# Batched 64x64 matmul: another order of issue for the b tiles, an early table load, a regroup in pieces and a store in halves

## The chip, the cores and the metric

One core of a Trainium2 chip runs the whole program. The metric is device time in microseconds (us), as the median of several executions. "Span" is the length of the one profiled execution, from its first to its last instruction; it is some 2 us shorter than the timed figure of the same program.

## The reference

```python
a = np.random.randn(1024, 64, 64).astype(np.float32)
b = np.random.randn(1024, 64, 64).astype(np.float32)
def reference(a, b):
    return np.matmul(a, b).astype(np.float32)
```

This reads 33.6 MB and writes 16.8 MB. The kernel computes in bf16: a is cast by its loads, b by ScalarE.

## The kernel before

b and the output are cut into 16 tiles t of 1.05 MB, a into 8 tiles s that serve two t each. The path of a tile of a: four loads issued by GpSimd (which cast it to bf16); a *regroup* on VectorE (DVE); transposes on TensorE; copies `at_sb` on ScalarE (ACT); then, for each t, four copies (*spread*) on DVE into a block-diagonal `at_bd`. b is loaded, then cast by ACT. TensorE leaves the products in PSUM; they are copied out of it (*evacuated*), first half of a tile by ACT and second half by DVE, and stored by GpSimd.

```python
    def load_b(t):
        b_sb = b_pool.tile([128, 16, 128], fp32, name="b_sb")       # 4 buffers
        queue = nc.scalar if t in (1, 3, 5, 7) else nc.sync
        load = queue.dma_start(out=b_sb[:], in_=b_v[t])
        # ... tiles 0 and 1 wait for the second piece of a tile 0 ...
    def regroup(s):
        # ...
        nc.vector.tensor_copy(a_bf[:], a_sb[:].rearrange("p h v k -> p v h k"))
    # ... in multiply(t), after the products:
            if not last:
                copy = nc.vector.tensor_copy if half else nc.scalar.copy
                evacuate(o_ps, 4 * half, 4, copy)
        if last:      # t == 15
            held[t] = [lambda q=q: put(2 * q, 2) for q in range(4)]
        else:
            held[t] = [lambda: put(0, 8)]
    # ... main loop (cut):
        for t in range(n_t):
            if t + 1 < n_t:
                spread(t + 1); cast(t + 1)
            if t + B_AHEAD < n_t:
                load_b(t + B_AHEAD)
            if half == 0:
                # ... regroup(s + 2), load_a(s + 4) ...
            multiply(t)
            # ... transpose ...
            if t >= HOLD - 1:
                store(t - HOLD + 1)
```

Every engine takes its instructions in this order. A load of b on ScalarE's queue therefore goes out only after the cast in front of it has got its data (in the prediction's lines a cast waits until 33.27 us, and the load of b tile 5 behind it goes out at 33.35). There are three DMA queues: q0 (loads of a and all stores, from GpSimd), q1 (b tiles from SyncE) and q10 (b tiles from ScalarE).

## Time and profile before

| | before |
|---|---|
| median of 4 runs | 137.08 us (136.76 to 137.43) |
| span of the profiled run | 134.8 us |
| busy: DVE, ACT, TensorE | 105.0, 84.5, 69.3 us |
| last store issued by GpSimd | 128.23 us (128.21 in the prediction, where the queue's own 0.02 us is counted in), landed 5.1 us later |

The slices, the stops of DVE and the queues are read in the prediction below. One view is shown here: how the end looks in single microseconds. The columns are the stretch, its length, the busy time of PE (TensorE), PEld (its weight loads), DVE, ACT and POOL (GpSimd) with numbers of instructions, TensorE's granted clock, the busy share of the 16 DMA engines and GB/s.

```profile
123.00:124.00 1.00, 1.00 (x24) 1.00 (x22) 0.97 (x3) 0.78 (x3) 0.00 (x0) 0.50 0.92 360
124.00:125.00 1.00, 0.45 (x9) 0.28 (x6) 0.96 (x3) 0.97 (x3) 0.04 (x1) 0.50 0.53 201
125.00:126.00 1.00, 0.00 (x0) 0.00 (x0) 0.97 (x3) 0.13 (x1) 1.00 (x2) 0.50 0.10 29
126.00:127.00 1.00, 0.00 (x0) 0.00 (x0) 0.96 (x3) 0.00 (x0) 1.00 (x2) 0.50 0.59 209
132.00:133.00 1.00, 0.00 (x0) 0.00 (x0) 0.00 (x0) 0.00 (x0) 0.00 (x0) 0.50 0.75 262
```

### The profile page before, as it was taken

The numbers are of one execution on the slowest core, as the hardware profiler recorded it, in microseconds if no ns is written. First come the engines' busy times: TensorE is split into PE (matmuls) and PEld (weight loads), VectorE is DVE, ScalarE is ACT, GpSimd is POOL, SyncE is SP. The second block draws the span as 40 slices with busy tenths as digits, with TensorE's granted clock in tenths as the row PEclk, the third lists the DMA queues.
The fourth block names the chain that finished last, engine by engine and source line by source line (L and its number), as shares of the span: only waits on it lengthen the run. The fifth ranks groups of instructions, "written<-read, shape, count | busy, mean of one in ns | idle before, by whom it ended". The sixth has DMA issues, their size and how long they took to land.

```text
span 134.8 us, 2815 instructions
## 1 busy us (share of the span) xinstructions
PE 69.3 (51%) x1152; PEld 65.2 (48%) x1152; DVE 105.0 (78%) x143; ACT 84.5 (63%) x122; POOL 46.6 (35%) x58
## 2 busy tenths in 40 slices
PE   0007305695169709389637861956039735669000
PEld 0007205695069609289637861956039625558000
DVE  5512099069999999997999999997599999999900
ACT  0010902992998995958996896699347996637100
POOL 6949723132413350152322243323021114040820
PEclk9999999999955995955995599599955995555555
DMA  2999999999999999999999999999999999998593
GB/s 19 185 204 261 309 305 301 309 308 279 272 294 311 312 394 346 303 275 361 393 360 273 272 381 396 340 267 288 393 394 396 393 399 395 407 406 350 191 320 136
DMA packets 17469, 42.12 MB, mean 312 GB/s; under 512 B 1073, under 2 KB 1073, under 8 KB 17457
## 3 DMA queue, kind: packets, MB, share of 16 engines
q0 software_dynamic: 9008, 25.17, 66.1%
q1 hardware_dynamic: 6336, 12.58, 26.0%
q10 hardware_dynamic: 2112, 4.19, 8.1%
q8 instruction: 9, 0.15, 0.4%
q14 instruction: 4, 0.02, 0.0%
HBM read 33.55 MB, written 16.78 MB: 373 GB/s over the span
## 4 chain that ended last, share of the span: by engine, by line
DMA 65%; DVE 18%; issue 9%; POOL 3%; POOLq 1%; DVEq 0%
DMA a_sb<-in_a_dram 48%; DMA out_dram<-o_sb 16%; DVE o_sb L157 10%; DVE at_bd L113 8%; POOL out_dram L146 2%; POOL a_sb L66 1%; POOLq L250 1%; DVE a_bf L91 0%; DVEq L91 0%; POOLq L146 0%; DVEq L113 0%; POOLq L239 0%
## 5 line engine op out<-in xcount | busy, mean ns | idle before, releaser
L169 PEld LDWEIGHTS <-at_bd 128*128 128x128 bf16 x1024 | 45.8, 117 | 41.4 <-DVE o_sb L157 30.7
L169 PE MATMUL o_ps<-b_bf,at_bd 128*128 128x64 bf16 x960 | 44.7, 219 | 36.6 <-DVE o_sb L157 28.7
L113 DVE COPY at_bd<-at_sb 32x1024 f32<-32x1024 f32 x64 | 46.4, 725 | 7.9 <-ACT at_sb L103 5.9
L157 DVE COPY o_sb<-o_ps 64x512 f32<-64x512 f32 x60 | 41.3, 688 | 1.8 <-PE o_ps L169 0.8
L157 ACT COPY o_sb<-o_ps 64x512 f32<-64x512 f32 x60 | 34.8, 580 | 9.5 <-DMA out_dram<-o_sb 5.3
L146 POOL DMA_DIRECT2D out_dram<-o_sb x19 | 21.0, 1107 | 46.9 <-DVE o_sb L157 20.1
L124 ACT CAST b_bf<-b_sb 128x2048 bf16<-128x2048 f32 x15 | 28.6, 1905 | 8.7 <-DMA b_sb<-in_b_dram 8.5
L66 POOL DMA_DIRECT2D a_sb<-in_a_dram x32 | 21.5, 681 | 35.2 <-DMA a_sb<-in_a_dram 21.0
L100 PE MATMUL at_ps<-identity,a_bf 128*128 128x128 f32 x128 | 24.4, 357 | 17.3 <-DVE a_bf L91 17.3
L100 PEld LDWEIGHTS at_ps<-identity,a_bf 128*128 128x128 f32 x128 | 20.5, 190 | 17.7 <-issue 17.7
L103 ACT COPY at_sb<-at_ps 128x512 f32<-128x512 f32 x32 | 17.6, 589 | 4.8 <-PE at_ps L100 4.5
L91 DVE COPY a_bf<-a_sb 128x4096 bf16<-128x4096 bf16 x8 | 9.8, 1228 | 11.5 <-DMA a_sb<-in_a_dram 11.3
L76 ACT MOVE_SHAPE b_sb<-in_b_dram x4 | 0.7, 172 | 7.9 <-DMA a_sb<-in_a_dram 7.0
L157 ACT COPY o_sb<-at_ps 64x256 f32<-64x256 f32 x8 | 2.9, 367 | 3.0 <-PE at_ps L169 2.9
L191 DVE MEMSET at_bd<- 128x4096 f32 x1 | 3.5, 3472 | 1.7 <-PEq L239 1.7
L103 ACT ACT_TABLE_LOAD x1 | 1.3, 1283 | 4.8 <-issue 4.8
L169 PE MATMUL at_ps<-b_bf,at_bd 128*128 128x64 bf16 x64 | 3.6, 241 | 1.2 <-DVE at_bd L113 1.2
L195 POOL MEMSET at_bd<- 128x4096 f32 x1 | 3.5, 3530 | 0.0
L157 DVE COPY o_sb<-at_ps 64x256 f32<-64x256 f32 x8 | 3.4, 421 | 0.1
L131 ACT CAST b_bf<-b_sb 128x512 bf16<-128x512 f32 x2 | 1.1, 615 | 1.9 <-DMA b_sb<-in_b_dram 1.9
L129 DVE CAST b_bf<-b_sb 128x512 bf16<-128x512 f32 x2 | 0.8, 424 | 0.0
masks.py:199 POOL TENSOR_SCALAR_AFFINE_SELECT identity<-identity 128x128 f32<-128x128 f32 x1 | 0.3, 287 | 0.1
(5 smaller groups left out, 0.6 us busy)
## 6 DMA issues: line engine op xcount, KB each, us to landing
out_dram<-o_sb POOLq DMA_DIRECT2D x15, 1024.0 KB, 21.8
a_sb<-in_a_dram POOLq DMA_DIRECT2D x32, 256.0 KB, 19.8
out_dram<-o_sb POOLq DMA_DIRECT2D x4, 256.0 KB, 5.3
b_sb<-in_b_dram SPq DMA_DIRECT2D x12, 0.5 KB, 18.3
b_sb<-in_b_dram ACTq DMA_DIRECT2D x4, 0.5 KB, 16.0
```

Source lines behind the costliest of these rows:

```text
L66: load = nc.gpsimd.dma_start(out=a_sb[:, h, :, :].rearrange("p v k -> p (v k)"), in_=a_v[s, h])
L91: nc.vector.tensor_copy(a_bf[:], a_sb[:].rearrange("p h v k -> p v h k"))
L100: nc.tensor.transpose(at_ps[:, vo, :], a_cols[:, 4 * vo + 2 * j + wl, :], identity[:])
L103: nc.scalar.copy(at_tiles[s][:, j, :, wl, :, :], at_ps[:].rearrange("p vo (g mp) -> p g mp vo", mp=4),)
L113: nc.vector.tensor_copy(bd[rows, :, :, :, h, :].rearrange("p j g wl mo -> p j (g wl) mo"), at_tiles[t // 2][rows, :, half, :, :, :].rearrange(
L124: nc.scalar.copy(b_bf[:], b_sb[:])
L146: nc.gpsimd.dma_start(out=o_v[t, :, lo : lo + n, :], in_=o_sb[:, lo : lo + n].rearrange("p gh j wl n -> p (gh j wl n)"),)
L157: copy(dst, src)
L169: nc.tensor.matmul(o_ps[:, gl, g % 2, j, :], at_bd[:, j, g, :, u], b_bf[:, g, 64 * u : 64 * u + 64], start=(u == 0), stop=(u == 1),)
L191: nc.vector.memset(bd_tiles[0][:], 0.0)
L195: nc.gpsimd.memset(bd_tiles[1][:], 0.0)
L250: with _tile.TileContext(nc) as tc:
```

## The change

The intent: free ScalarE at the head (its second load of b held it for 4.77 us, and its table load came after that), start the transposes of the first tile earlier, and let half of tile 14 be stored before DVE has evacuated the rest.

```diff
+    warm = consts.tile([128, 2], fp32)
@@ load_b
-        queue = nc.scalar if t in (1, 3, 5, 7) else nc.sync
+        queue = nc.scalar if t in (1, 4, 6, 7) else nc.sync
@@ regroup
-        nc.vector.tensor_copy(a_bf[:], a_sb[:].rearrange("p h v k -> p v h k"))
+        for lo, hi in [(0, 1), (1, 2), (2, 3), (3, 4)] if s == 0 else [(0, 4)]:
+            nc.vector.tensor_copy(
+                a_bf[:, :, lo:hi, :],
+                a_sb[:, lo:hi, :, :].rearrange("p h v k -> p v h k"),
+            )
@@ multiply
-            held[t] = [lambda: put(0, 8)]
+            whole = t < n_t - 2
+            held[t] = [lambda q=q: put(q, 8 if whole else 4) for q in ([0] if whole else [0, 4])]
@@ after load_a(0)
+        nc.vector.memset(warm[:, 0:1], 0.0)
+        nc.scalar.copy(warm[:, 1:2], warm[:, 0:1])
```

## The prediction

> **What bounds the kernel now.** I read the page's forty slices first, to see which resource is full and when.
>
> ```profile
> DVE  5512099069999999997999999997599999999900
> ACT  0010902992998995958996896699347996637100
> DMA  2999999999999999999999999999999999998593
> ```
>
> A slice is 134.8 / 40 = 3.37 us. The DMA row is full from slice 1 to slice 35, about 3.4 to 121 us; DVE is nearly full from slice 9 to slice 37; ACT is not. So a shorter instruction pays only if it fills an empty DMA slice or moves the DVE stream. Next, the timeline of DVE, for the places where it stops. Columns: start, length, instruction, in brackets the idle time before it and what ended it.
>
> ```profile
> 9.60 1.23 DVE L91 COPY a_bf<-a_sb 128x4096 bf16<-128x4096 bf16 x1 [4.47 <-DMA a_sb<-in_a_dram]
> 16.75 2.83 DVE L113 COPY at_bd<-at_sb 32x1024 f32<-32x1024 f32 x4 [5.92 <-ACT at_sb L103]
> 28.10 1.23 DVE L91 COPY a_bf<-a_sb 128x4096 bf16<-128x4096 bf16 x1 [4.51 <-DMA a_sb<-in_a_dram]
> 45.18 2.83 DVE L113 COPY at_bd<-at_sb 32x1024 f32<-32x1024 f32 x4
> 95.80 1.23 DVE L91 COPY a_bf<-a_sb 128x4096 bf16<-128x4096 bf16 x1 [2.33 <-DMA a_sb<-in_a_dram]
> 124.45 3.48 DVE L157 COPY o_sb<-at_ps 64x256 f32<-64x256 f32 x8
> ```
>
> After 28.1 us DVE runs to 127.93 us with one large stop, 2.33 us at 95.80, for the last tile of a (tile 7). From there 32.1 us of DVE work follow, almost without a gap, then the last stores. The end is therefore: landing of a tile 7, plus 32.1 us, plus the tail of the stores. Third, ScalarE at the head:
>
> ```profile
> 8.56 4.77 ACTq L76 DMA_DIRECT2D b_sb<-in_b_dram  x1
> 13.37 1.28 ACT L103 ACT_TABLE_LOAD   x1 [4.83 <-issue]
> 22.72 1.90 ACT L124 CAST b_bf<-b_sb 128x2048 bf16<-128x2048 f32 x1 [6.01 <-DMA b_sb<-in_b_dram]
> 33.27 1.90 ACT L124 CAST b_bf<-b_sb 128x2048 bf16<-128x2048 f32 x1 [2.54 <-DMA b_sb<-in_b_dram]
> ```
>
> ACT is held 4.77 us by issuing b tile 3 and then loads its table, but a little later it waits 6.01 us for b tile 0 anyway. Fourth, the DMA queues in 1 us stretches (packets, MB, share), 43 to 44 us and then 33 to 34 us:
>
> ```profile
> q0 software_dynamic: 50, 0.09, 45.6%
> q1 hardware_dynamic: 54, 0.11, 31.8%
> q10 hardware_dynamic: 52, 0.11, 27.3%
> ...
> q0 software_dynamic: 67, 0.13, 70.0%
> q1 hardware_dynamic: 66, 0.14, 39.5%
> q10 hardware_dynamic: 1, 0.00, 0.1%
> ```
>
> q0 carries a and the stores, q1 the b tiles of SyncE, q10 those of ScalarE. Queues with work get equal numbers of packets: with q10 empty, q0 gets 67 per us instead of 50. Last, the stretches of the end (length; PE, PEld, DVE, ACT, POOL; clock, DMA share, GB/s):
>
> ```profile
> 114.00:120.00 6.00, 3.78 (x64) 3.46 (x64) 5.80 (x9) 3.46 (x6) 1.36 (x1) 0.50 1.03 405
> 120.00:125.00 5.00, 3.59 (x64) 3.43 (x64) 4.82 (x10) 2.80 (x8) 0.04 (x1) 0.50 0.90 352
> 125.00:128.20 3.20, 0.00 (x0) 0.00 (x0) 2.83 (x7) 0.13 (x1) 2.97 (x4) 0.50 0.59 200
> ```
>
> Here is the hole: before the last two stores the DMA falls to 200 GB/s (in single microseconds 201, 29 and 209 from 124 to 127), because the store of tile 14 is issued whole at 124.97.
>
> **What the Trainium skill says.** "DMA: Bandwidth & Descriptors", section "Queues, rings and completion order": each DMA engine goes round robin between the queues with work, by packet. The trace agrees (50, 54, 52; then 67, 66). Same page, "Latency and other measured facts": about 600 ns to the first byte on the SyncE/ScalarE path. This trace differs: b tile 5 was issued on ScalarE at 33.35 and q10 moved no data before about 37.9, some 4.5 us; b tiles 0 and 1 (issued 7.03) started at about 11.5. I use 4.5. "ScalarE: Activation LUTs", "What ACT_TABLE_LOAD costs": about 1283 ns; the trace has 1283. "VectorE: DVE Perf Modes", "Side-by-side: where the cycles go": a 4x bf16 copy costs elements/4 plus about 158 cycles at 0.96 GHz; 4096 elements make 1231 ns, the trace has 1228. A quarter should cost 414 / 0.96 = 431 ns (an estimate from that section).
>
> **The change, part by part.**
>
> 1. *Table early.* One tiny memset and copy are added; the 1.28 us load moves into ACT's first 7 us, where it is idle. 2. *Four-piece regroup.* 1.23 us becomes 4 x 0.43 us, three of them while later pieces of the tile still land. Transposes can start about 10.1 instead of 10.98. 3. *b tile 3 to SyncE:* ACT loses its 4.77 us block. Together the four copies of at_sb end near 14.4 instead of 16.71, since the 16 transposes take 3.65 us and the last copy 0.6; spread 0 ends near 17.3 instead of 19.58. None of this reaches the end by itself: the first products still need b tile 0 (landed 22.7) and its cast (24.6), and DVE still stops for a tile 2. So I put 0 us on parts 1 and 2.
>
> 4. *The new order of b.* Before: q1 has 0, 2, 4, 6, 8...; q10 has 1, 3, 5, 7. After: q1 has 0, 2, 3, 5, 8...; q10 has 1, 4, 6, 7. Data of b tiles 0 and 1 is through by about 22. Tile 4 can be issued by ACT only beside its second cast (25.5), with data at about 30, so q10 is empty for 8 us where tile 3 now follows at once. Then q0 moves about 70 packets per us instead of 50: the last two pieces of a tile 2 (256 packets) take 3.7 instead of 5.1 us, and it lands near 26.5 instead of 28.0. b tile 2 has q1's larger share too and lands near 30 instead of 33.2. DVE restarts about 1.2 us earlier (its next evacuation needs products that end at 28.1).
>
> The price: b tile 3 is now behind tile 2 on q1 and shares with tile 4, at 33 packets per engine and 52/16 = 3.25 per us: 10.2 us, landing near 40.4 (its cast was at 38.42). ACT works in order: cast 1.9, four evacuations 2.4, two at_sb copies 1.1, so spread 4 starts near 46 instead of 45.18. DVE ends that passage 0.8 us late. It has 2.33 us of slack at 95.8.
>
> Over the whole run, q10 is busy beside q1 for fewer microseconds: before 11.5 to 32.1 and 37.9 to 59.1, 41.8 us; after about 11.5 to 22, 30 to 40.4, 45 to 49 and 52 to 65, some 38 us. In each of the 4 us saved q0 moves 18 packets more; 72 packets at 68 per us are 1.1 us. a tile 7 lands near 94.6, DVE is ready for it near 94.3, and the last 32.1 us begin about 1.1 us earlier.
>
> 5. *Tile 14 in halves.* Its first half (0.52 MB) is evacuated by ACT at 119.19 and can be issued then, 5 us ahead. It fills the hole: 0.52 MB no longer stand behind 124.97, at the 340 GB/s of the last stores 1.5 us. One DVE spread then coincides with a store's issue and stretches from 0.69 to 0.95 us (as others do now): +0.26.
>
> Sum: -1.1 - 1.5 + 0.3 = -2.3 us, 134.7. I put 134.8, as such gains seldom come whole.
>
> **The rivals.** (a) *Only the tail counts:* the late b tile 3 and the early a tiles cancel; a tile 7 lands as now, because the DMA is full and moves the same bytes. Then -1.2: 135.8. For it: the full DMA row. Against: the equal shares, which favour q0 when q10 is empty. (b) *The wait for b tile 3 takes the place of the removed one:* ACT stops for 4 to 5 us, evacuations and stores shift, and the 2.33 us of slack do not cover it, +1 in place of -1.1: about 136.8. For it: only 1 us lies between the last at_sb copy (44.15) and spread 4 (45.18). (c) *All is recovered:* the DMA never runs dry at the end, which the hole of about 0.76 MB against 400 GB/s allows, 1.9 us, and the start comes 1.5 us earlier: 133.6. (d) *Everything hidden,* because the last piece of tile 15, issued at 128.21 and gated by DVE, sets the end and not the queue ahead of it. Against: its 5.1 us from issue to landing are mostly queue. 137.
>
> **Range and chances.** (a) and the sum are likeliest, (c) less so, (b) and (d) least. That spans 133.4 to 136.4. The line for faster is 0.98 x 137.04 = 134.3, half a microsecond under my figure: 0.34. Slower than 139.8 needs a wait nothing shows: 0.02.
>
> **What would show it.** Part 1 to 3: ACT's table load before 7 us, at_sb copies ended near 14.4, and still a wait for b tile 0 until about 22.7. Part 4: DVE's regroup of a tile 2 near 26.6, ACT's fourth cast waiting for DMA until about 40.5, spread 4 near 46, the regroup of a tile 7 near 94.7. Part 5: a store issued near 119 and no microsecond under 300 GB/s between 120 and 128. I am wrong if the fourth cast waits much beyond 42 and DVE reaches a tile 7 later than 95.8, or if the last stretch from DVE's end to the end of the span (6.9 us) does not shrink.

## The result, and the profile after

| | before | changed |
|---|---|---|
| median | 137.08 us (4 runs) | 135.59 us (4 runs, 135.51 to 135.68) |
| ratio | | 0.9891, 95% interval 0.9865 to 0.9916 |
| span of the profiled run | 134.8 us | 133.8 us |
| DVE starts the last regroup (a tile 7) | 95.80 us | 94.98 us |
| DVE ends | 127.93 us | 127.14 us |
| last store issued | 128.23 us | 127.43 us |

A ratio here is the mean time of one kernel's runs over that of the other's of the same rounds, so it is not quite the ratio of the medians. The change is worth 1.5 us (1.1%): within 2%, and in the range. The figure forecast was 134.8.

The timeline of DVE in the changed kernel, the lines that answer to those of the prediction:

```profile
9.41 0.43 DVE L94 COPY a_bf<-a_sb 128x1024 bf16<-128x1024 bf16 x1 [0.82 <-DMA a_sb<-in_a_dram]
14.29 2.83 DVE L119 COPY at_bd<-at_sb 32x1024 f32<-32x1024 f32 x4 [4.45 <-ACT at_sb L109]
26.97 1.23 DVE L94 COPY a_bf<-a_sb 128x4096 bf16<-128x4096 bf16 x1 [5.39 <-DMA a_sb<-in_a_dram]
45.71 3.15 DVE L119 COPY at_bd<-at_sb 32x1024 f32<-32x1024 f32 x4 [1.81 <-ACT at_sb L109]
94.98 1.23 DVE L94 COPY a_bf<-a_sb 128x4096 bf16<-128x4096 bf16 x1 [1.53 <-DMA a_sb<-in_a_dram]
123.65 3.49 DVE L163 COPY o_sb<-at_ps 64x256 f32<-64x256 f32 x8
```

The first spread is 2.5 us earlier, and DVE waits the longer for a tile 2, which comes 1.1 us earlier. At 45.71 there is a new stop of 1.81 us. The last regroup starts 0.8 us earlier. ScalarE in the changed kernel:

```profile
0.74 1.28 ACT L198 ACT_TABLE_LOAD   x1 [0.74 <-PEq L249]
22.47 1.90 ACT L130 CAST b_bf<-b_sb 128x2048 bf16<-128x2048 f32 x1 [8.21 <-DMA b_sb<-in_b_dram]
40.42 1.90 ACT L130 CAST b_bf<-b_sb 128x2048 bf16<-128x2048 f32 x1 [4.73 <-DMA b_sb<-in_b_dram]
117.92 1.14 ACT L137 CAST b_bf<-b_sb 128x512 bf16<-128x512 f32 x2 [3.68 <-DMA b_sb<-in_b_dram]
```

The table load is out of the way of the copies of `at_sb`, and the wait for b tile 0 has grown from 6.01 to 8.21 us: the time saved at the head went into that wait. The fourth line is one that the prediction did not have: b tile 15 arrives at 117.9 instead of 115.2. The queues of the changed kernel from 25 to 26 us, where before all three had 49 packets each:

```profile
q0 software_dynamic: 74, 0.12, 66.3%
q1 hardware_dynamic: 73, 0.15, 42.8%
```

q10 is empty here, as b tile 4 was issued at 24.45 and no packet of it moved before 28.6. Last the end, GpSimd's issues of stores and then the stretches (columns as above):

```profile
121.73 0.77 POOL L152 DMA_DIRECT2D out_dram<-o_sb  x1 [2.94 <-ACT o_sb L163]
123.91 1.46 POOL L152 DMA_DIRECT2D out_dram<-o_sb  x2 [1.42 <-DVE o_sb L163]
125.67 1.43 POOL L152 DMA_DIRECT2D out_dram<-o_sb  x2 [0.30 <-DVE o_sb L163]
127.43 0.72 POOL L152 DMA_DIRECT2D out_dram<-o_sb  x1 [0.33 <-DVE o_sb L163]
```

```profile
125.00:126.00 1.00, 0.00 (x0) 0.00 (x0) 0.95 (x3) 0.00 (x0) 0.69 (x2) 0.50 0.95 361
130.00:131.00 1.00, 0.00 (x0) 0.00 (x0) 0.00 (x0) 0.00 (x0) 0.00 (x0) 0.50 0.45 172
131.00:132.00 1.00, 0.00 (x0) 0.00 (x0) 0.00 (x0) 0.00 (x0) 0.00 (x0) 0.50 0.05 20
```

The hole is closed (29 GB/s have become 361). Most DMA engines end before 131. After that the share is 0.05: of 16 engines, 0.05 x 16 = 0.8, so about one engine works on alone for a microsecond, and the program waits for it. The packed trace, read packet by packet, agrees: from 130.91 us on there is one chain of packets of 4096 bytes, each 0.164 or 0.165 us long and begun as the one before it ends, until 131.88. From the last issue to the end of the span it is 6.4 us, where it was 6.6.

### The profile page after: what moved, and what is told of

It is laid out like the page before. It is cut to its first block, busy times and chain, and to the rows that moved or that the text cites. A ratio compares the mean times of both kernels' runs of the same rounds, so it can differ in the third digit from the quotient of the medians.

```text
span 133.8 us, 2818 instructions
## 1 busy us (share of the span) xinstructions
PE 68.8 (51%) x1152; PEld 64.0 (48%) x1152; DVE 105.7 (79%) x147; ACT 84.6 (63%) x123; POOL 45.4 (34%) x59
## 4 chain that ended last, share of the span: by engine, by line
DMA 64%; DVE 14%; issue 11%; POOL 4%; POOLq 1%; DVEq 0%
DMA a_sb<-in_a_dram 49%; DMA out_dram<-o_sb 15%; DVE o_sb L163 8%; DVE at_bd L119 6%; POOL out_dram L152 3%; POOL a_sb L67 1%; DVE a_bf L94 1%; POOLq L260 1%; DVEq L94 0%; POOLq L152 0%; DVEq L119 0%; POOLq L249 0%
## 5 line engine op out<-in xcount | busy, mean ns | idle before, releaser
L175 PEld LDWEIGHTS <-at_bd 128*128 128x128 bf16 x1024 | 44.7, 115 | 43.9 <-DVE o_sb L163 26.5
L175 PE MATMUL o_ps<-b_bf,at_bd 128*128 128x64 bf16 x960 | 43.7, 217 | 38.3 <-DVE o_sb L163 24.1
L130 ACT CAST b_bf<-b_sb 128x2048 bf16<-128x2048 f32 x15 | 28.6, 1905 | 16.5 <-DMA b_sb<-in_b_dram 16.5
L152 POOL DMA_DIRECT2D out_dram<-o_sb x20 | 20.1, 1005 | 48.0 <-DVE o_sb L163 18.4
L94 DVE COPY a_bf<-a_sb 128x4096 bf16<-128x4096 bf16 (+1 forms) x11 | 10.6, 959 | 10.5 <-DMA a_sb<-in_a_dram 10.4
L77 ACT MOVE_SHAPE b_sb<-in_b_dram x4 | 0.1, 24 | 4.7 <-DMA a_sb<-in_a_dram 4.7
```

The source lines that it names most:

```text
L94: nc.vector.tensor_copy(a_bf[:, :, lo:hi, :], a_sb[:, lo:hi, :, :].rearrange("p h v k -> p v h k"),)
L130: nc.scalar.copy(b_bf[:], b_sb[:])
L152: nc.gpsimd.dma_start(out=o_v[t, :, lo : lo + n, :], in_=o_sb[:, lo : lo + n].rearrange("p gh j wl n -> p (gh j wl n)"),)
L175: nc.tensor.matmul(o_ps[:, gl, g % 2, j, :], at_bd[:, j, g, :, u], b_bf[:, g, 64 * u : 64 * u + 64], start=(u == 0), stop=(u == 1),)
```

## The experiments

**My theory after the result:** the new order of b brings the last a tile 0.8 us forward, the halves close the hole, the head is worth nothing; and the two gains do not add, since with the hole closed the DMA engines' own work sets the end. **Rivals:** the head has a share; the new order costs as much as it brings (by the late b tile 3); the end is set by the last store's issue plus a fixed delay.

| run | median us | ratio to before (95%) |
|---|---|---|
| order of b alone | 136.42 | 0.9952 (0.9916 to 0.9988) |
| halves alone | 135.79 | 0.9910 (0.9882 to 0.9938) |
| head alone | 136.83 | 0.9994 (0.9954 to 1.0033) |
| order and halves | 135.87 | 0.9910 (0.9890 to 0.9930) |
| odd b tiles on ScalarE throughout | 139.94 | 1.0194 (1.0140 to 1.0247) |
| all b tiles on SyncE | 142.87 | 1.0415 (1.0388 to 1.0441) |
| changed, last quarter by ScalarE | 135.72 | 0.9891 (0.9870 to 0.9913) |
| changed, b tile 4 on SyncE too | 136.09 | 0.9912 (0.9886 to 0.9938) |
| changed, tile 15 in halves | 135.57 | 0.9886 (0.9857 to 0.9916) |
| changed kernel again | 135.46 | 0.9876 (0.9850 to 0.9902) |
| changed, tile 10 not stored | 134.28 | 0.9776 (0.9742 to 0.9810) |
| the same, last quarter by ScalarE | 134.28 | 0.9774 (0.9738 to 0.9810) |

The first four runs shared a chip and the runs of the kernel before; so did the next four, the next two, and the last two.

### The parts of the change, one at a time

Order alone, an edit of the kernel before:

```diff
-        queue = nc.scalar if t in (1, 3, 5, 7) else nc.sync
+        queue = nc.scalar if t in (1, 4, 6, 7) else nc.sync
```

> The new order of b alone, everything else as in the kernel before. Theory: a tile 7 lands about 0.8 us earlier (94.98 in the changed kernel, 95.80 before), so DVE ends 0.8 us earlier, and b tile 15 lands near 117, late enough that the backlog of stores fills the hole of 124 to 127 us by itself: 0.7 to 1.2 us faster than before. Rival 'the order only pays with the halves': within 0.3 us of before. Rival 'the late fourth b tile costs': slower than before by 0.5 us or more.

0.0048 x 137.1 = 0.66 us faster, just under the range that the theory gave. The last regroup starts at 95.11, the last store is issued at 127.55, so the whole chain has moved by 0.7 us and the end with it (span 134.1). The hole is shorter but still there (213 and 131 GB/s from 124 to 126): the later b tile 15 did not fill it, as I had expected it to. The interval reaches from 0.2 to 1.2 us, so the times alone do not quite exclude the rival's 0.3.

Halves alone, an edit of the kernel before:

```diff
-            held[t] = [lambda: put(0, 8)]
+            whole = t < n_t - 2
+            held[t] = [lambda q=q: put(q, 8 if whole else 4) for q in ([0] if whole else [0, 4])]
```

> Tile 14 stored in halves alone. Theory: a tile 7 lands as before (95.8), the first half is issued near 119.5 and fills the hole; the bulk of the DMA ends about 1.5 us earlier, but the last landing is held by the last piece (issued 128.2) and by a DMA engine that lags: 0.5 to 1.0 us faster. Rival of the prediction's sum: 1.2 us or more faster. Rival 'the last piece sets the end': within 0.2 us of before.

0.0090 x 137.1 = 1.2 us faster, above the 0.5 to 1.0 of the theory and as much as the rival asked for. DVE's last regroup and GpSimd's issues of stores in that run:

```profile
95.93 1.23 DVE L91 COPY a_bf<-a_sb 128x4096 bf16<-128x4096 bf16 x1 [1.94 <-DMA a_sb<-in_a_dram]
...
118.36 2.16 POOL L146 DMA_DIRECT2D out_dram<-o_sb  x2 [4.58 <-issue]
...
128.45 0.72 POOL L146 DMA_DIRECT2D out_dram<-o_sb  x1 [0.34 <-DVE o_sb L157]
```

The first half of tile 14 goes out behind tile 13's store. DVE's last stretch starts at 95.93, no earlier than before, and the last store goes out at 128.45, a full microsecond later than in the changed kernel; yet its span is 133.7 against the changed kernel's 133.8. This is the main finding, and the run of order and halves below, which differs from this one by the order alone, repeats it: with the hole closed, one microsecond of DVE more or less does not show at the end. The last piece landed 3.8 us after its issue here and 4.9 us after it in the changed kernel.

The head alone: the changed kernel with `(1, 3, 5, 7)` and `put(0, 8)` put back.

> The early table load and the regroup in four pieces alone, order of b and stores as before. Theory: copies of at_sb end a little earlier, all of it hidden by the wait for b tile 0 and a tile 2: within 0.2 us of before. Rival 'the head counts': 0.5 us or more faster.

No difference is shown (0.9994), but the interval reaches from 0.6 us faster to 0.5 us slower. One of the six runs, the profiled one, took 138.44, and in it a tile 2 was regrouped at 30.89 instead of 28.10; the others took 136.5 to 137.0, 136.77 in the mean, 0.4 us below the 137.17 of the kernel before. So the head may be worth anything from nothing to about 0.4 us; the rival's 0.5 us or more is not seen, and the theory's 0.2 is not confirmed.

Order and halves without the head: both edits above on the kernel before.

> New order of b and halves of tile 14, without the early table and the four pieces. Theory: the same time as the whole change within 0.2 us, 135.4 to 135.8. Rival 'the head counts once the order has freed ScalarE': 0.5 us or more slower than the whole change.

135.87, the same ratio as the halves alone (0.9910). The same two lines in that run:

```profile
94.88 1.23 DVE L91 COPY a_bf<-a_sb 128x4096 bf16<-128x4096 bf16 x1 [1.06 <-DMA a_sb<-in_a_dram]
...
127.31 0.72 POOL L146 DMA_DIRECT2D out_dram<-o_sb  x1 [0.34 <-DVE o_sb L157]
```

Both come 1.1 us earlier than with the halves alone, but the span is 133.7 again. So on top of the halves, the order brings nothing that these runs can see. The whole change is 0.3 to 0.4 us below this run (135.59 and 135.46), a little more than the theory's 0.2, with overlapping intervals; the run of the head alone allows as much, but whether the head brings it is not settled.

### Is it the sharing of the DMA between queues?

Two extreme orders, each an edit of the changed kernel:

```diff
-        queue = nc.scalar if t in (1, 4, 6, 7) else nc.sync
+        queue = nc.scalar if t % 2 else nc.sync        # first run
+        queue = nc.sync                                # second run
```

> The changed kernel with every odd b tile, to the last, issued by ScalarE: two b queues stay in work beside the queue of a and the stores. Theory of equal shares by packet: b tile 15 lands well before 117 (near 105 to 110), a tile 7 lands 2 to 5 us later than 94.9, and DVE's last stretch with it: 2 to 4 us slower than the changed kernel. Rival 'the issuing queue does not matter, the DMA moves the same bytes': within 0.5 us.

> The changed kernel with all b tiles issued by SyncE: one b queue only. Theory of equal shares: b tile 1 lands behind tile 0, near 27 instead of 22.8, a tile 2 lands earlier (near 23 to 25 instead of 26.9), b becomes what ScalarE waits for all along and b tile 15 lands past 120: 3 to 8 us slower. Rival 'less time with three queues is always better': faster by up to 1 us.

The first: 4.4 us slower than the changed kernel, a little more than forecast. DVE's timeline at its last regroup:

```profile
99.81 1.23 DVE L94 COPY a_bf<-a_sb 128x4096 bf16<-128x4096 bf16 x1 [3.81 <-DMA a_sb<-in_a_dram]
```

a tile 7 is regrouped 4.8 us later: both b queues stay in work up to that moment (in the packed trace q1 until 99.9 us, and q10 until 107.7, where b tile 15 landed, in the 105 to 110 forecast). The second: 7.3 us slower. DVE's regroup of a tile 2 and ScalarE's second cast in that run:

```profile
24.35 1.23 DVE L94 COPY a_bf<-a_sb 128x4096 bf16<-128x4096 bf16 x1 [3.22 <-DMA a_sb<-in_a_dram]
```

```profile
27.24 1.90 ACT L130 CAST b_bf<-b_sb 128x2048 bf16<-128x2048 f32 x1 [4.57 <-DMA b_sb<-in_b_dram]
```

a tile 2 comes 2.6 us earlier than in the changed kernel, b tile 1 near 27, and ScalarE waits for b at each of the first twelve casts. Both rivals fall: the queue that issues b decides how the DMA is split between a and b, and it can be wrong in either direction. The cast of b tile 15 at 122.4 did not wait, but its last packet moved at 120.6 in the packed trace, past 120 as forecast.

### Was it the late fourth b tile?

```diff
-        queue = nc.scalar if t in (1, 4, 6, 7) else nc.sync
+        queue = nc.scalar if t in (1, 6, 7) else nc.sync
```

> The changed kernel with b tile 4 on SyncE too, behind tile 3, so that tile 3 has a two-queue share and lands near 38 instead of 40.4. Theory: DVE's stop of 1.8 us at the fifth spread goes and a tile 7 lands a little earlier, but the end is held by the DMA: within 0.4 us of the changed kernel. Rival 'the stop for b tile 3 is what ate the gain': 1 us faster or more.

The stop at the fifth spread is gone and the fourth cast starts at 37.28, but ScalarE now waits 5.04 us for a b tile at 55.99, and DVE stops 2.94 us at 61.27. The time is 136.09: no gain. But the run put a longer stop in place of the one that it removed, and DVE starts its last regroup at 95.85 without a wait for the DMA, later than the 94.98 of the changed kernel and not earlier as forecast. So it does not settle what the stop itself costs; against the rival speaks the main finding, not this run. The last store went out at 128.29, 0.9 us later than in the changed kernel, and the span is 133.7 once more.

### What sets the end?

The last quarter of tile 15 evacuated by ScalarE:

```diff
-                    copy = nc.scalar.copy if g8 == 3 else nc.vector.tensor_copy
+                    copy = nc.scalar.copy if g8 == 3 or g == 15 else nc.vector.tensor_copy
```

> The changed kernel with the last quarter of tile 15 evacuated by ScalarE instead of DVE, so that the last store is issued about 1.1 us earlier (126.3 instead of 127.4). Theory: with the hole filled, the end is set by the DMA engines, one of which lags by 1 us, and not by the last issue: within 0.3 us of the changed kernel. Rival 'the last issue sets the end': 0.8 to 1.1 us faster than it.

GpSimd's last issues in that run:

```profile
125.42 2.14 POOL L152 DMA_DIRECT2D out_dram<-o_sb  x3 [0.30 <-DVE o_sb L163]
```

Three issues of 0.71 us each: the last one starts near 126.8, so it came only 0.6 us earlier, not 1.1, because GpSimd issues one store after another. The time is the same as the changed kernel's (135.72).

Then tile 15 in two halves, with that edit kept, and the changed kernel itself for comparison:

```diff
-            held[t] = [lambda q=q: put(2 * q, 2) for q in range(4)]
+            held[t] = [lambda q=q: put(4 * q, 4) for q in range(2)]
```

> The changed kernel with tile 15 stored in two halves (rows of 4 KB) instead of four quarters (rows of 2 KB), and its last quarter evacuated by ScalarE so that the second half is issued near 126.5. Theory: the end is set by the DMA engines' bytes; quarters moved at about 350 GB/s, halves at about 400, which saves 1.05 MB x (1/350 - 1/400), 0.4 us: 0.2 to 0.5 us faster than the changed kernel of the same call. Rival 'the last issue sets the end': about 1 us faster. Rival 'row size does not matter': the same.

> The changed kernel itself, in the same call for comparison and as a check on its spread: 135.4 to 135.9, and again one DMA engine at work a microsecond after the others.

135.57 and 135.46: no gain from longer rows, so my 0.4 us was wrong. In both runs a single engine's worth of packets moves after 131 us, as in the changed kernel.

The last two runs leave out the store of tile 10, with a wrong result, in the changed kernel and in the one with the last quarter on ScalarE:

```diff
         for piece in held.pop(t):
-            piece()
+            if t != 10:
+                piece()
```

> The changed kernel without the store of tile 10 (the result is wrong on purpose): 1.05 MB less for the DMA before the end, every instruction of the compute engines as it was. Theory 'the DMA engines' work sets the end': the backlog is gone, the last landing follows the last issue (about 127.4) by less than now, the lone late engine disappears, 0.8 to 2.2 us faster than the changed kernel. Rival 'a fixed delay after the last issue, some 6.3 us, sets the end': within 0.3 us of the changed kernel.

> The same with the last quarter of tile 15 evacuated by ScalarE (wrong on purpose too). Theory: with the DMA relieved, the last issue is the bound, so the earlier last issue that was worth nothing before now shows: 0.3 to 1 us faster than the run without it. Rival 'DMA still full': the same time as that run.

1.2 to 1.3 us faster than the changed kernel by the medians, 1.4 to 1.6 by the ratios. GpSimd's last issue in the first of the two:

```profile
127.78 0.72 POOL L153 DMA_DIRECT2D out_dram<-o_sb  x1 [0.34 <-DVE o_sb L164]
```

It is 0.35 us later than in the changed kernel, and the span ends at 132.5, 4.7 us after it instead of 6.4. The piece landed 3.2 us after its issue instead of 4.9, and no packet moves after 131. So the delay after the last issue is not fixed: taking 1.05 MB from the DMA takes 1.7 us from it, and at least that much of it was queue. What the other 3.2 us to the landing are, these runs do not show. The fixed-delay rival falls. The hole is open again in this run (156 and 172 GB/s from 124 to 126), so not all of the 1.05 MB could be gained. The last run was to show that the last issue is then the bound. It does not test it: its last three issues were again one behind another, the last near 128.0, no earlier than the 127.78 of the run before, and its time is the same. That part is left open.

The packed traces show one thing more. In the seven runs of about the changed kernel's time with the hole closed (the changed kernel twice, halves alone, order and halves, last quarter by ScalarE, b tile 4 on SyncE too, tile 15 in halves), the last packet of all ends at 131.6 to 131.9 us, whether the last store was issued at 126.8, 127.3, 127.4, 128.3 or 128.45. The rest does follow the issue: apart from one last chain of packets like that of the changed kernel, data ends by 131.0 where the last issue was at 127.4 or earlier and at 131.5 after the two late ones. So a microsecond of DVE moves the bulk of the DMA engines and not the last one, and the program waits for the last. In the runs with a hole (before, order alone, head alone, the two extreme orders, and the two without the store of tile 10) no such chain is left over.

## Why the prediction was right or wrong

The time lies within the range and within 2% of the kernel before; the figure of 134.8 was 0.8 us too low. Step by step:

- *"So I put 0 us on parts 1 and 2."* Not contradicted: 0.9994 alone, but up to about 0.4 us is not excluded. The copies of `at_sb` ended at 14.3 (14.4 forecast), and ScalarE then waited for b tile 0 until 22.47 (22.7 forecast).
- *Equal shares.* Right: with q10 empty, q0 had 66 to 74 packets per us from 22 to 28 us; a tile 2 was regrouped at 26.97 (near 26.6 forecast), the fourth cast waited until 40.42 (40.5), spread 4 started at 45.71 (46). The two extreme orders confirm the mechanism. One sum came near by luck: in the packed trace the time with both b queues in work fell from 42.2 to 38.6 us (41.8 to 38 forecast), but q10 was in work for 41.7 us after the change, and most of the saving was a gap of q1, from 48.6 to 51.8 us, which the prediction did not have.
- *"the last 32.1 us begin about 1.1 us earlier."* The size was 0.8 us in the trace, and 0.66 in the time of the order alone: this term was mis-sized by about 0.4 us.
- *The tail, "1.5 us" and "+0.26".* The net 1.2 us is what the halves alone brought. The 0.26 hardly came: DVE's last stretch took 32.2 us with the halves, where it had taken 32.1. In the changed kernel the half was issued at 121.73 and not at 119, because ScalarE's cast of b tile 15 stood in front of its evacuation and waited until 117.92. I had not carried the order of b through to tile 15: q1 had no b packets from 49 to 51 us (b tile 5 had landed, tile 8 was issued at 47.56), and b tile 15, on that queue, came 2.7 us later than before.
- *"Sum: -1.1 - 1.5 + 0.3 = -2.3 us"* is the step that failed. Each term was worth something alone, 0.7 and 1.2 us, but they do not add to 1.9: order and halves together gave 1.2. The intervals of these times are wide (0.2 to 1.2, 0.8 to 1.6 and 1.0 to 1.5 us); the traces say it more clearly. Both gains come out of the hole, which had been idle DMA time. Added up from the busy shares of the ten microseconds from 120 to 130, the DMA idled for 1.9 us before, 1.1 with the order alone, 0.4 with the halves alone and 0.1 with both, so the two took 0.8 and 1.5 us out of 1.9. The order's earlier DVE work pays only as long as the end waits for DVE; once the hole is closed it waits for the DMA, which is at 90% or more in every slice from about 3 us to 130. The bulk of the data did end some 2 us earlier (before 131 instead of at 133), as the sum says, but one engine's worth went on to 131.9, and the program ends with the last engine. Of the 0.8 us by which 134.8 was too low, about half is the mis-sized term above, and the rest is that the two do not add. The prediction's own sign of being wrong, that the stretch from DVE's end to the end of the span does not shrink, all but came: it went from 6.9 to 6.7 us. Its other sign for the tail held, as no microsecond from 120 to 128 fell under 348 GB/s.
- *Rival (a), "Only the tail counts"*, had the best time, 135.8, and half of its reason: a tile 7 did land earlier, but the DMA, being full, did not let it count. *Rival (d)* asked whether the last issue sets the end; the run without one store answers that 1.7 of the 4.9 us to its landing are queue; that they are "mostly queue", as I had argued against it, is not shown. *Rival (b)* had the new stop right (1.81 us at 45.71), but the slack at a tile 7 covered it: DVE still waited 1.53 us there. *Rival (c)* needed the gains to add.

Left open: which engine is last and why it lags; what the stop at 45.71 costs; whether the head is worth the 0.3 us by which the whole change beats order and halves.

## What to carry to other kernels

Count the idle DMA time first: where the DMA is full from start to end, as here, the hole that is left (1.9 us here) is about all that an earlier compute engine or an earlier store could win, and savings counted one by one are not to be added beyond it. When tiles go through several DMA queues, work out the shares over the whole run, to the last tile, for moving one early load can make the last one late. And look at the end by engines, not by GB/s: the program waits for the last of sixteen.

## What the Trainium skill lacked or had wrong

- "DMA: Bandwidth & Descriptors", "Issuing engines are not separate DMA queues", says that issuing from several engines only saves the sequencer's issue time. The total is indeed shared, but which data comes first is not neutral: all b tiles on SyncE 142.87 us, alternating 139.94, the changed order 135.5.
- The same page, "Latency and other measured facts", has about 600 ns to the first byte on the SyncE/ScalarE path. Here a 1 MB load with 512-byte rows took 4.2 to 4.5 us from its issue to its first packet, before (33.35 to 37.84) and after (24.45 to 28.61).
- The same section says that two of the sixteen engines are usually slower. It gives no figure. Here one engine's worth of packets (share 0.05 of 16 engines) moved for 0.7 to 1 us after the others had ended, in both profiled runs of the changed kernel; the trace does not name the engine.
